# A third Strassen group in the down products of a macaron layer's first SwiGLU, with its post-norm moved to ScalarE

## Chip, cores and metric

The kernel runs on one core of a Trainium2 chip, as one launch. The metric is the device time of the launch in microseconds (us). The engines are called PE (TensorE), DVE (VectorE), ACT (ScalarE), POOL (GpSimd) and SP (SyncE).

## What is computed

One hybrid decoder layer on 256 tokens of width 1024 in float32. Cut to what matters here:

```python
def rmsnorm(x, g):
    return x * lax.rsqrt(jnp.mean(x * x, axis=-1, keepdims=True) + EPS) * g

def swiglu(x, w_gate, w_up, w_down):            # w_gate, w_up: 1024 x 2816; w_down: 2816 x 1024
    return (jax.nn.silu(x @ w_gate) * (x @ w_up)) @ w_down

h = h + 0.5 * rmsnorm(swiglu(rmsnorm(h, ffn1_pre_g), ...ffn1...), ffn1_post_g)
u = rmsnorm(h, mix_pre_g)
# the mixer: u @ w_in, a Mamba-2 branch and a differential attention branch, gated, merged, w_out
h = h + rmsnorm(merged @ w_out, mix_post_g)
h = h + 0.5 * rmsnorm(swiglu(rmsnorm(h, ffn2_pre_g), ...ffn2...), ffn2_post_g)
```

The change touches the first SwiGLU ("f1"), its post-norm, and the step from there to the mixer ("mx"). The last SwiGLU ("f2") runs through the same functions.

## The kernel before

**Numbers.** Every product is made of three: each operand is split into a high part (rounded to fp32r by a cast, mostly on ACT) and a low part (the rest, by a subtraction on DVE); high x high, low x high and high x low are accumulated in PSUM. Weights stream from HBM in chunks of 1 MB: SP issues the load into one of three `raw` tiles (`load_to`), two casts on ACT make `whi` (line 251) and two subtractions on DVE make `wlo` (line 254). Once a chunk is split, its raw tile is free, and the load of the third chunk behind it is issued. `take` hands out the next weights and first splits up to three chunks ahead (`AHEAD`).

**Down products.** The 2816 rows of w_down are 11 chunks of 256 rows. In the plan string `DOWN`, "p" is a plain chunk: 2 k-tiles x 2 token blocks x 3 terms x 2 halves of the columns. "q" with a digit is a Strassen group of two chunks: seven products (Winograd's form) instead of eight, each 2 k-tiles x 3 terms of 128 x 512. Its weight operands are four quarters of the two chunks and four sums of them (`Quad.sum_of`, line 123, on DVE); each of the seven operands is split (`wqh`, line 131, on ACT; `wql`, line 136, on DVE). Its activation operands are also sums (`sums_of`), made on DVE while the gate and up products run. `mm_quads` runs the plan up to the last group (line 629), in seven PSUM banks. `combine` adds the banks up on ACT and DVE. `mm_n` (line 577) does the plain chunks behind the last group; it holds the last three (`TAIL`) and does them in the order block 0 left half, block 0 right half, block 1 left, block 1 right, so that block 0 can be normed while block 1 is multiplied.

**Post-norm and the next norm.** When a block of 128 tokens is done, `done` adds the combined parts (line 789) and calls `post_norm`: squares summed on ACT (line 446), a product with the gain on DVE (`og`, line 545), 1/rms, and the update of h on DVE (line 554). 1/rms is `rstd_of` on POOL (lines 451 and 452: an add and a power of -0.5); only the last SwiGLU, where `ready is store`, makes it on ACT as exp(-0.5 ln(x)). Then comes the mixer's norm: the sum of squares of h and 1/rms on POOL (`r_mx`), for block 1 the scaled `un_mx` (line 505), transposes on PE (`pu_mx`, line 460), and their casts and low parts (`u_mx`, lines 466 and 468). Block 0's transposes stand on PE between the left and the right half of block 1. The mixer's first products (`pn_mx`, line 336) are four of 12 matmuls for block 0, with block 1's transposes behind the third, then four for block 1.

**Order.** Tile, the framework, places the instructions of ACT, DVE, POOL and SP (and PE where no order is given) by program order and readiness; each engine then runs its queue in order. From the held chunks to the end of the mixer's first products PE's order is the written one. `add_manual_dep` with `order` is an edge that only bends the order of the queues. In `mm_n` the weights of later chunks are split at two places: up to two chunks ahead behind block 0's norm (`split_to(ahead_of(taken[0], AHEAD - 1))`) and up to three behind block 1's products. ACT has one table of functions loaded at a time; `act_table(EXP_LN)` loads the one with Ln and Exp.

Of the kernel before, what the change touches and what calls it, by code (L numbers as in the profile page):

```python
# [16 lines left out]
F32 = mybir.dt.float32  # L17
F32R = mybir.dt.float32r
AF = mybir.ActivationFunctionType
ALU = mybir.AluOpType  # L20
# [3 lines left out]
EXP_LN = "natural_log_exp_and_others"  # L24
# [16 lines left out]
AHEAD = 3  # L41
# [4 lines left out]
QK_US = 2.4  # L46
GATE_US = 1.75
SSD_US = 1.55
DOWN = {"f1": "p q1 p p q2 p ppp", "f2": "q1 p q2 p q3 ppp"}
FIRST, LAST = (1, 2, 3, 5, 7, 6, 4), (1, 6, 7, 2, 5, 3, 4)  # L50
BREAK, STOP = object(), object()

# [2 lines left out]
def tile_hybrid_layer(ctx: ExitStack, tc: tile.TileContext, x, ffn1_pre_g, ffn1_w_gate, ffn1_w_up,  # L55
# [4 lines left out]
    nc = tc.nc  # L60
# [157 lines left out]
    ffn_chunks("f2", ffn2_w_gate, ffn2_w_up, ffn2_w_down)  # L218

    raws, splits = [], []  # L220
    taken = [0]

    def load_to(n):
# [9 lines left out]
    def split_steps(ahead=True):  # L233


        i, _ = units[len(splits)]
        load_to(i + 1)
        r, shape = raws[i], chunks[i][1]
        nj = shape[1] // 2
        his, los = [], []  # L240
        splits.append((his, los))
        for q in range(2):
            hi = k4([P, nj, shape[2]], f"whi{i}{q}", F32R)
            lo = k4([P, nj, shape[2]], f"wlo{i}{q}", F32R)
            his.append(hi)
            los.append(lo)
            n = 1 if i == 0 else nj
            for j in range(0, nj, n):
                js = slice(j, j + n)
                copy = nc.scalar.copy if i + q + j else nc.vector.tensor_copy  # L250
                copy(hi[:, js, :], r[:, q * nj + j:q * nj + j + n, :])  # L251
                if not i + q + j:
                    yield
                nc.vector.tensor_sub(lo[:, js, :], r[:, q * nj + j:q * nj + j + n, :], hi[:, js, :].bitcast(F32))  # L254
                yield
        raws[i] = None
        if ahead:
            load_to(i + 1 + RAW_BUFS)

    def split_to(n):  # L260

        while len(splits) < min(n, len(units)):
            of, p = units[len(splits)]
            if p is not None:
                splits.append(of.split(p))
                continue
            for _ in split_steps():
                pass

    def ahead_of(i, n):  # L270

        n *= 4
        while n > 0 and i < len(units):
            n -= 4 if units[i][1] is None else 1
            i += 1
        return i
# [72 lines left out]
                between[i + 1]()  # L349


    act_since, act_fence = [], [None]
    order = mybir.DependencyInfo(mybir.DependencyClass.NoSync, mybir.DependencyReason.DATA)

    def act_table(name):
        f = nc.scalar.preload_act_table_set(name)
        for prev in act_since:
            tc.add_manual_dep(f.ins, prev, order, reason="activation table")
        act_since.clear()
        act_fence[0] = f.ins.name  # L360

    def act(*args, **kw):
        a = nc.scalar.activation(*args, **kw)
        if act_fence[0] is not None:
            tc.add_manual_dep(a.ins, act_fence[0], order, reason="activation table")
        act_since.append(a.ins.name)


    order_of, ordered = [ExitStack()], [False]
# [162 lines left out]
        for q in range(2):  # L532
            split(*in_u(b)(q), us[q])

    def post_norm(b, acc, pg, fold, tag, last=False):

        ss = tiny(2, f"sp_{tag}{b}")
        og = []
        for q in range(2):
            sum_sq(ss[:, q:q + 1], acc[q], fold, f"jp_{tag}{b}{q}")  # L540
            if last and q == 0:
                e = tiny(1, f"ep_{tag}{b}")
                nc.vector.tensor_scalar(e, ss[:, 0:1], fold * EPS, None, ALU.add)
            og.append(k2([P, 512], f"og_{tag}{b}{q}"))
            nc.vector.tensor_tensor(og[q], acc[q], pg[:, halves[q]], ALU.mult)
        if last:
            r = tiny(1, f"rp_{tag}{b}")
            act(r, ss[:, 1:2], AF.Ln, bias=e)
            act(r, r, AF.Exp, scale=-0.5)
        else:  # L550
            r = rstd_of(ss, fold, f"rp_{tag}{b}")
        for q in range(2):
            hq = h[:, b, halves[q]]
            nc.vector.scalar_tensor_tensor(hq, og[q], r, hq, ALU.mult, ALU.add)

    def load_gain(v, name):
        pg = k4([P, D], name)
# [3 lines left out]
    def mm_n(acc, acts, ready, turned, begun=lambda: None, pairs=None, begin=True, taken_all=lambda: None):  # L561

        pairs = pairs or range(len(acts) // 2)
        n = len(pairs)
        held = []

        def one(i, w, parts):
            wh, wl = w  # L570
            for kt in range(2):
                ah, al = acts[2 * pairs[i] + kt]
                for b, qs in parts:
                    ts = slice(b * P, (b + 1) * P)
                    for x_, w_ in ((ah, wh), (al, wh), (ah, wl)):
                        for q in qs:
                            nc.tensor.matmul(acc[b][q], x_[:, ts], w_(kt)[:, halves[q]],  # L577
                                             start=begin and i == 0 and kt == 0 and x_ is ah and w_ is wh,
                                             stop=i == n - 1 and kt == 1 and w_ is wl)
                if i == 0:  # L580
                    begun()

        for i in range(n):
            w = take(min(n - i, AHEAD))
            if i < n - TAIL:
                one(i, w, ((0, (0, 1)), (1, (0, 1))))
            else:
                held.append((i, w))
        taken_all()
        own_order(PE)  # L590
        for q in range(2):
            for i, w in held:
                one(i, w, ((0, (q,)),))
        ready(0)
        split_to(ahead_of(taken[0], AHEAD - 1))
        for q in range(2):
            for i, w in held:
                if q == 1 and i == n - TAIL:
                    turned()
                one(i, w, ((1, (q,)),))  # L600
        split_to(ahead_of(taken[0], AHEAD))
        ready(1)

    def sums_of(g, even, odd):

# [129 lines left out]
    def ffn(post_v, tag, ready, turned, then, products):  # L735
        gu = []

        gh = k4([P, 4, T], f"gh_{tag}0", F32R)
        gl = k4([P, 4, T], f"gl_{tag}0", F32R)
        gu += [(gh[:, m, :], gl[:, m, :]) for m in range(4)]  # L740
        sgs = []

        def evict(b, i, acc, r):
            if i == 0:
                sgs.append(k2([P, 512], f"sg_{tag}b{b}"))
                act(sgs[b], acc, AF.Silu, scale=1.0 if r is None else r)
            elif r is None:
                nc.vector.tensor_tensor(sgs[b], acc, sgs[b], ALU.mult)
            else:
                nc.vector.scalar_tensor_tensor(sgs[b], acc, r, sgs[b], ALU.mult, ALU.mult)  # L750

        def back(b):
            bs = slice(b * P, (b + 1) * P)
            pt_ = bg([P, 4, P], f"pt_{tag}{b}")
            for m in range(4):
                nc.tensor.transpose(pt_[:, m, :], sgs[b][:, m * P:(m + 1) * P], ident)
            split(gh[:, :, bs], gl[:, :, bs], pt_)

        products(evict, back)
        back(1)  # L760
        del sgs
        then()
        sums = {}
        for j in range(2, FF // T):
            if j % 2 == 0:
                gh = k4([P, 4, T], f"gh_{tag}{j}", F32R)
                gl = k4([P, 4, T], f"gl_{tag}{j}", F32R)
            o = (j % 2) * 2
            gu += [(gh[:, o + m, :], gl[:, o + m, :]) for m in range(2)]
            sg = k2([P, 2, T], f"sg_{tag}{j}")  # L770
            mm_w(sg, f"pg_{tag}{j}", take(), act_u)
            act(sg, sg, AF.Silu)
            su = k2([P, 2, T], f"su_{tag}{j}")
            mm_w(su, f"pup_{tag}{j}", take(), act_u)
            nc.vector.tensor_tensor(sg, su, sg, ALU.mult)  # L775
            split(gh[:, o:o + 2, :], gl[:, o:o + 2, :], sg)
            if j // 2 in QUADS[tag]:
                if j % 2:
                    sums[j // 2] = sums_of(j // 2, even, sg)
                else:  # L780
                    even = sg
        if ready is store:
            act_table(EXP_LN)
        acc, rest, combine, pairs = mm_quads(gu, sums, tag)
        pg = load_gain(post_v, f"pg_{tag}")

        def done(b):
            for q in range(2):
                nc.vector.tensor_tensor(rest[b][q], acc[b][q], rest[b][q], ALU.add)
            post_norm(b, rest[b], pg, 4.0, tag, ready is store)  # L790
            ready(b)

        mm_n(acc, gu, done, turned, pairs=pairs, begin=False,
             taken_all=combine)

# [176 lines left out]
    pol = const.tile(shp, F32, name="dtp")  # L972
    dt = const.tile(shp, F32, name="dt")

    act_table(EXP_LN)

    lp = const.tile([P, 2, 64], F32, name="lp")
    lvv = lv.rearrange("p (a b) d -> p a b d", b=2)
# [503 lines left out]
```

## Time and profile before

| | us |
|---|---|
| median of 3 runs (lowest to highest) | 735.31 (735.09 to 735.91) |
| profiled execution, its own time | 735.79 |
| its span, from the first instruction to the last | 734.1 |
| PE busy (mean granted clock 0.998) | 725.8 |
| DVE busy | 598.9 |
| ACT busy | 469.4 |

A row of a timeline is: start (us from the span's start), length, engine, line, operation, tiles written <- read, shapes, count, and in brackets the idle time before it and what ended it. A row of the chain of waits, which is followed back from the last instruction, is: start, length, engine, tile, line, count. Tiles are named without their numbers: `acc_f1p` are the down products' banks of the first SwiGLU, `acc_f2p` those of the last.

### The profile page before, as it was taken

The numbers are of one execution on the slowest core, as the hardware profiler recorded it, in microseconds if no ns is written. First come the engines' busy times: TensorE is split into PE (matmuls) and PEld (weight loads), VectorE is DVE, ScalarE is ACT, GpSimd is POOL, SyncE is SP. The second block draws the span as 40 slices with busy tenths as digits, with TensorE's granted clock in tenths as the row PEclk, the third lists the DMA queues.
The fourth block names the chain that finished last, engine by engine and source line by source line (L and its number), as shares of the span: only waits on it lengthen the run. The fifth ranks groups of instructions, "written<-read, shape, count | busy, mean of one in ns | idle before, by whom it ended". The sixth has DMA issues, their size and how long they took to land.

```text
span 734.1 us, 10540 instructions
## 1 busy us (share of the span) xinstructions
PE 725.8 (99%) x4025; PEld 619.3 (84%) x4025; DVE 598.9 (82%) x929; ACT 469.4 (64%) x801; POOL 38.6 (5%) x72
## 2 busy tenths in 40 slices
PE   9999999999999999999999999999999999999996
PEld 7888888888878889999888788888888888888875
DVE  6978777999679999777996997784774878779994
ACT  6666566655567676869965577772663657566562
POOL 2800000000300000000000000000010000000000
PEclk9999999999999999999999999999999999999999
DMA  8874664459353647656564664364460664664541
GB/s 290 239 248 155 225 232 173 129 220 370 119 172 118 191 153 242 212 168 211 157 221 148 208 213 149 138 248 183 135 241 26 230 206 154 214 221 146 185 166 57
DMA packets 94210, 137.92 MB, mean 188 GB/s; under 512 B 2684, under 2 KB 68304, under 8 KB 94160
## 3 DMA queue, kind: packets, MB, share of 16 engines
q1 hardware_dynamic: 91488, 129.51, 52.1%
q0 software_dynamic: 2368, 7.22, 3.1%
q8 instruction: 31, 0.51, 0.3%
q10 hardware_dynamic: 304, 0.53, 0.2%
q14 instruction: 19, 0.16, 0.1%
HBM read 136.17 MB, written 1.08 MB: 187 GB/s over the span
## 4 chain that ended last, share of the span: by engine, by line
PE 97%; DVE 1%; DMA 1%; issue 1%; ACT 0%; SPq 0%; DVEq 0%
PE pup_f L317 9%; PE pg_f L317 9%; PE pws L336 6%; PE pgt L336 6%; PE acc_f1p L629 5%; PE acc_f2p L629 5%; PE pg_f L316 4%; PE pxs L317 4%; PE pup_f L316 4%; PE pn_f L346 3%; PE pn_mx L336 3%; PE acc_mx L577 3%; PE pn_f L336 3%; PE pwd L336 3%; PE acc_f1p L577 3%; PE pz L302 2%
## 5 line engine op out<-in xcount | busy, mean ns | idle before, releaser
L254 DVE TENSOR_TENSOR wlo<-raw,whi 128x1024 fp32r<-128x1024 f32 (+1 forms) x226 | 267.1, 1211 | 21.1 <-ACT whi L251 19.9
L251 ACT CAST whi<-raw 128x1024 fp32r<-128x1024 f32 (+1 forms) x225 | 226.9, 1045 | 15.7 <-DMA raw<-in_w_in_dram 3.4
L317 PE MATMUL pg_f<-u_f,whi 128*128 128x512 f32 x288 | 101.3, 396 | 0.0
L317 PE MATMUL pup_f<-u_f,whi 128*128 128x512 f32 x288 | 101.3, 396 | 0.0
L316 PE MATMUL pg_f<-u_f,wlo 128*128 128x256 f32 x252 | 70.6, 280 | 0.0
L316 PE MATMUL pup_f<-u_f,wlo 128*128 128x256 f32 x252 | 70.3, 279 | 0.0
L317 PEld LDWEIGHTS pup_f<-u_f,whi 128*128 128x128 f32 x288 | 52.8, 188 | 9.8
L317 PEld LDWEIGHTS pg_f<-u_f,whi 128*128 128x128 f32 x288 | 52.8, 188 | 9.7
L316 PEld LDWEIGHTS pg_f<-u_f,wlo 128*128 128x128 f32 x252 | 47.5, 189 | 1.7
L316 PEld LDWEIGHTS pup_f<-u_f,wlo 128*128 128x128 f32 x252 | 47.5, 188 | 1.6
L317 PE MATMUL pxs<-u_mx,whi 128*128 128x512 f32 x128 | 44.6, 397 | 0.0
L322 DVE TENSOR_TENSOR su_f<-pup_f,su_f 128x256 f32<-128x256 f32 x36 | 15.2, 422 | 26.7 <-ACT su_f L321 26.6
L321 ACT COPY su_f<-pup_f 128x256 f32<-128x256 f32 x36 | 13.3, 370 | 36.1 <-PE pup_f L317 35.9
L131 ACT CAST wqh<-wt 128x1024 fp32r<-128x1024 f32 x20 | 21.1, 1054 | 22.8 <-DVE wt L123 17.8
L336 PE MATMUL pgt<-whi,u_mx 128*128 128x512 f32 x128 | 33.1, 393 | 0.0
L302 PE MATMUL pz<-u_mx,whi 128*128 128x256 f32 x128 | 31.8, 285 | 0.0
L303 PE MATMUL pz<-u_mx,whi 128*128 128x256 f32 x128 | 31.4, 283 | 0.0
L316 PE MATMUL pxs<-u_mx,wlo 128*128 128x256 f32 x112 | 31.2, 279 | 0.0
L336 PEld LDWEIGHTS pgt<-whi,u_mx 128*128 128x128 f32 x128 | 23.6, 188 | 5.4 <-issue 0.7
L317 PEld LDWEIGHTS pxs<-u_mx,whi 128*128 128x128 f32 x128 | 23.2, 188 | 4.2
L302 PEld LDWEIGHTS pz<-u_mx,whi 128*128 128x128 f32 x128 | 24.5, 191 | 0.2 <-issue 0.2
L292 ACT CAST gh_f<-sg_f 128x512 fp32r<-128x512 f32 x18 | 11.2, 621 | 21.0 <-DVE sg_f L775 21.0
(402 smaller groups left out, 1681.2 us busy)
## 6 DMA issues: line engine op xcount, KB each, us to landing
raw<-in_w_in_dram SPq DMA_DIRECT2D x40, 1024.0 KB, 5.1
raw<-in_ffn_w_down_dram SPq DMA_DIRECT2D x22, 1024.0 KB, 4.7
raw<-in_ffn_w_gate_dram SPq DMA_DIRECT2D x20, 1024.0 KB, 5.1
raw<-in_ffn_w_up_dram SPq DMA_DIRECT2D x20, 1024.0 KB, 5.0
raw<-in_ssd_w_branch_dram SPq DMA_DIRECT2D x8, 1024.0 KB, 4.8
acb<-acd POOLq DMA_DIRECT2D x8, 512.0 KB, 4.3
raw<-in_da_w_branch_dram SPq DMA_DIRECT2D x4, 1024.0 KB, 4.9
raw<-in_w_out_dram SPq DMA_DIRECT2D x4, 1024.0 KB, 4.8
```

The costliest lines, as they stand in the source:

```text
L131: nc.scalar.copy(hi, src)
L251: copy(hi[:, js, :], r[:, q * nj + j:q * nj + j + n, :])
L254: nc.vector.tensor_sub(lo[:, js, :], r[:, q * nj + j:q * nj + j + n, :], hi[:, js, :].bitcast(F32))
L302: nc.tensor.matmul(acc[m], wh(j)[:, cs], ah(k0 + j), start=first and j == ks[0], stop=False)
L303: nc.tensor.matmul(acc[m], wh(j)[:, cs], al(k0 + j), start=False, stop=False)
L316: nc.tensor.matmul(acc[:, :T], wl(j)[:, cs], ah(j), start=False, stop=False)
L317: nc.tensor.matmul(acc, wh(j)[:, cs], ahl(j), start=j == 0, stop=j == KD - 1)
L322: nc.vector.tensor_tensor(dst[:, m, :], acc[:, :T], dst[:, m, :], ALU.add)
L336: nc.tensor.matmul(acc, a(k0 + j), b(j), start=first and i == 0, stop=last and i == 11)
L346: nc.tensor.matmul(accs[b], x_(k0 + j), w_(j), start=first and j == 0 and w_ is wh and x_ is acts[b][0], stop=last and j == 3 and w_ is wl)
L577: nc.tensor.matmul(acc[b][q], x_[:, ts], w_(kt)[:, halves[q]], start=begin and i == 0 and kt == 0 and x_ is ah and w_ is wh, stop=i == n - ...
L629: nc.tensor.matmul(bank[p], x_, w_, start=p not in begun, stop=last and p in (1, 5, 6, 7))
```

## The change

The first SwiGLU's plan becomes that of the last: three groups and five plain chunks instead of two and seven, the first group first, and three plain chunks behind the last group instead of four. `post_norm` of both SwiGLUs makes 1/rms by Ln and Exp on ACT; the table load for it is written ahead of the down products of both, and the one that was written later, ahead of the mixer's dt, is gone. In `mm_n` the splits behind block 0's norm fall into two: one chunk ahead without a fence, and the second with its low parts behind block 0's last update of h. The third chunk's low parts are behind that too, and its casts behind block 0's Exp. Block 1's adds (`done`) are behind block 0's last update as well. The mixer's own post-norm (`mxp`) stays on POOL and sets no fence.

```diff
-DOWN = {"f1": "p q1 p p q2 p ppp", "f2": "q1 p q2 p q3 ppp"}
+DOWN = {"f1": "q1 p q2 p q3 ppp", "f2": "q1 p q2 p q3 ppp"}
...
+    normed = {"lo": None, "cast": None}
+    def behind(m, what):
+        if normed[what] is not None:
+            tc.add_manual_dep(m.ins, normed[what].name, order, reason="behind a norm")
+        return m
...
-                copy(hi[:, js, :], r[:, q * nj + j:q * nj + j + n, :])
+                behind(copy(hi[:, js, :], r[:, q * nj + j:q * nj + j + n, :]), "cast")
...
-                nc.vector.tensor_sub(lo[:, js, :], r[:, q * nj + j:q * nj + j + n, :], hi[:, js, :].bitcast(F32))
+                behind(nc.vector.tensor_sub(lo[:, js, :], r[:, q * nj + j:q * nj + j + n, :],
+                                            hi[:, js, :].bitcast(F32)), "lo")
...
-    def post_norm(b, acc, pg, fold, tag, last=False):
+    def post_norm(b, acc, pg, fold, tag, scalar=False):
...
-        if last:
+        if scalar:
             r = tiny(1, f"rp_{tag}{b}")
             act(r, ss[:, 1:2], AF.Ln, bias=e)
             act(r, r, AF.Exp, scale=-0.5)
+            last_norm["cast"] = act_last[0]
         else:
             r = rstd_of(ss, fold, f"rp_{tag}{b}")
         for q in range(2):
             hq = h[:, b, halves[q]]
-            nc.vector.scalar_tensor_tensor(hq, og[q], r, hq, ALU.mult, ALU.add)
+            m = nc.vector.scalar_tensor_tensor(hq, og[q], r, hq, ALU.mult, ALU.add)
+            if scalar:
+                last_norm["lo"] = m.ins
...
         ready(0)
+        split_to(ahead_of(taken[0], AHEAD - 2))
+        normed["lo"] = last_norm.get("lo")
         split_to(ahead_of(taken[0], AHEAD - 1))
+        normed.update(last_norm)
...
         split_to(ahead_of(taken[0], AHEAD))
         ready(1)
+        normed.update(lo=None, cast=None)
+        last_norm.clear()
...
-        if ready is store:
-            act_table(EXP_LN)
+        act_table(EXP_LN)
...
-                nc.vector.tensor_tensor(rest[b][q], acc[b][q], rest[b][q], ALU.add)
-            post_norm(b, rest[b], pg, 4.0, tag, ready is store)
+                behind(nc.vector.tensor_tensor(rest[b][q], acc[b][q], rest[b][q], ALU.add), "lo")
+            post_norm(b, rest[b], pg, 4.0, tag, True)
...
-    act_table(EXP_LN)
```

More of the change, by code (lines that the diff above doesn't have):

```diff
@@ L349, in mm_both @@
                 between[i + 1]()
-    act_since, act_fence = [], [None]
+    act_since, act_fence, act_last, last_norm = [], [None], [None], {}
     order = mybir.DependencyInfo(mybir.DependencyClass.NoSync, mybir.DependencyReason.DATA)
@@ L366, in act @@
         act_since.append(a.ins.name)
+        act_last[0] = a.ins
     order_of, ordered = [ExitStack()], [False]
@@ L540, in post_norm @@
             sum_sq(ss[:, q:q + 1], acc[q], fold, f"jp_{tag}{b}{q}")
-            if last and q == 0:
+            if scalar and q == 0:
                 e = tiny(1, f"ep_{tag}{b}")
```

## The prediction

> **What bounds the kernel now.** I read the page's busy line first, then the chain of waits around the two down stages, then the timelines of VectorE (DVE) and ScalarE (ACT) there.
>
> ```profile
> span 734.1 us, 10540 instructions
> PE 725.8 (99%) x4025; PEld 619.3 (84%) x4025; DVE 598.9 (82%) x929; ACT 469.4 (64%) x801; POOL 38.6 (5%) x72
> ...
> 133.40 35.36 PE acc_f1p L629 x156
> 168.76 17.68 PE acc_f1p L577 x78
> 186.45 0.87 PE pu_mx L460 x8
> 187.32 4.10 PE acc_f1p L577 x18
> 191.52 8.23 PE pn_mx L336 x36
> 199.75 0.88 PE pu_mx L460 x8
> 200.62 5.48 PE pn_mx L336 x24
> 206.32 8.20 PE pn_mx L336 x36
> ```
>
> TensorE (PE) is busy for 99% of the span. In the chain, the first SwiGLU's down products (L629, then L577) and the mixer's first products (L336) follow each other with no other engine between them. 156 matmuls in 35.36 us are 0.2267 us each; that pitch, not the modelled duration of one matmul, is the price of one. Before the change this stretch has no stall to win back. Time is saved only by giving PE fewer matmuls, and is lost only by making PE wait.
>
> The second SwiGLU (f2) runs today with the plan that the first is to get. Its chain is the nearest thing to a trace of the change:
>
> ```profile
> 671.18 33.35 PE acc_f2p L629 x147
> 704.57 1.26 DVE wql L136 x2
> ...
> 713.19 1.23 DVE wlo L254
> 714.46 12.78 PE acc_f2p L577 x55
> ...
> 710.02 0.39 PE L577 MATMUL acc_f2p<-whi,gh_f 128*128 128x512 f32 x1
> 714.46 0.50 PE L577 MATMUL acc_f2p<-wlo,gh_f 128*128 128x512 f32 x1 [0.17 <-DVE wlo L254]
> 726.84 0.39 PE L577 MATMUL acc_f2p<-wlo,gh_f 128*128 128x512 f32 x1
> ```
>
> Here the chain leaves PE and runs through DVE from 704.57 to 714.46: the low parts of the weights (wql, wlo) are made only just in time, and the last is late.
>
> **Matmuls.** A plain chunk is 24 matmuls (2 k-tiles, 2 token blocks, 3 terms, 2 halves), a group of two chunks 48. A Strassen group is 7 products of 2 k-tiles by 3 terms, 42. One more group takes 6 matmuls out (252 become 246): 6 x 0.2267 = 1.36 us off PE's path. That is the whole expected gain. The Trainium skill's TensorE: Matmul & The Clock Gate ("Wait — 56ns, not 53.3ns?") measures 215.7 ns start to start for 512 columns; by it the gain would be 1.29. The trace's 0.2267 decides.
>
> **What the group adds on DVE and ACT.** Seven splits stand in place of four: three more casts on ACT, three more low parts and four weight sums (L123) on DVE.
>
> ```profile
> 136.35 1.22 DVE L123 TENSOR_TENSOR wt<-raw,wt 128x1024 f32<-128x1024 f32 x1
> 137.48 1.22 DVE L136 TENSOR_TENSOR wql<-wt,wqh 128x1024 fp32r<-128x1024 f32 x1
> 138.62 1.22 DVE L123 TENSOR_TENSOR wt<-raw,wt 128x1024 f32<-128x1024 f32 x1
> 706.91 4.63 DVE L254 TENSOR_TENSOR wlo<-raw,whi 128x1024 fp32r<-128x1024 f32 x4
> 711.46 0.69 DVE L658 TENSOR_TENSOR u_f<-acc_f2p,p_f 128x512 f32<-128x512 f32 x1
> 712.06 2.35 DVE L254 TENSOR_TENSOR wlo<-raw,whi 128x1024 fp32r<-128x1024 f32 x2
> 710.57 2.00 ACT L251 CAST whi<-raw 128x1024 fp32r<-128x1024 f32 x2 [1.02 <-DMA raw<-in_ffn_w_down_dram]
> ```
>
> The starts are 1.135 us apart, so seven more DVE operations are 7.95 us. They lie beside PE's work only while DVE keeps ahead. In f2 it doesn't quite: between 710.02 and the last start plus one pitch (726.84 + 0.23 = 727.07) lie 17.05 us, and 72 matmuls at 0.2267 are 16.32. The loss is **0.73 us**. It is the last plain chunk's low parts (712.06 x2), held up by its load (ACT sat 1.02 us for it; the load could start only when DVE had released the last group's raw tile) and by the combine's sum at 711.46. The first SwiGLU gets the same plan, buffers and look-ahead, so I charge these 0.73 us there. The bounds are 0 (today's first SwiGLU shows none) and 0.73 plus what the tail below adds.
>
> The activation sums of the third group are hidden. Gate and up products start 11.19 us apart both in the first SwiGLU at a place without sums and in f2 where group 3's are made:
>
> ```profile
> 113.61 0.47 PE pg_f L317 x2
> 124.80 0.47 PE pg_f L317 x2
> 639.71 0.46 PE pg_f L317 x2
> 650.89 0.46 PE pg_f L317 x2
> ```
>
> I cost them at nothing. DMA moves the same bytes. The table load is written earlier but stays one load, so it is also nothing.
>
> **The post-norm.** Two POOL operations per block go; a one-column add on DVE, Ln and Exp come.
>
> ```profile
> 182.40 0.69 DVE L789 TENSOR_TENSOR u_f<-acc_f1p,u_f 128x512 f32<-128x512 f32 x1 [0.39 <-PE acc_f1p L577]
> 185.02 1.42 DVE L554 SCALAR_TENSOR_TENSOR h<-og_f,rp_f,h 128x512 f32<-128x512 f32 x2 [1.20 <-POOL rp_f L452]
> 192.05 0.69 DVE L789 TENSOR_TENSOR c_f<-acc_f1p,c_f 128x512 f32<-128x512 f32 x1
> 195.49 1.42 DVE L554 SCALAR_TENSOR_TENSOR h<-og_f,rp_f,h 128x512 f32<-128x512 f32 x2 [0.84 <-POOL rp_f L452]
> 198.80 1.02 DVE L505 TENSOR_SCALAR un_mx<-h,r_mx 128x512 f32<-128x512 f32 x2 [1.89 <-POOL r_mx L452]
> 719.10 0.69 DVE L789 TENSOR_TENSOR u_f<-acc_f2p,u_f 128x512 f32<-128x512 f32 x1 [1.36 <-PE acc_f2p L577]
> 721.14 1.42 DVE L554 SCALAR_TENSOR_TENSOR h<-og_f,rp_f,h 128x512 f32<-128x512 f32 x2 [0.62 <-ACT rp_f L363]
> 193.65 1.17 POOL L451 TENSOR_SCALAR rp_f<-sp_f 128x1 f32<-128x1 f32 x1 [4.93 <-ACT jp_f L446]
> 197.82 0.30 POOL L451 TENSOR_SCALAR r_mx<-ss_mx 128x1 f32<-128x1 f32 x1 [2.37 <-ACT sq_mx L446]
> 186.40:199.80 13.40, 13.40 (x66) 11.13 (x65) 9.74 (x20) 8.10 (x23) 4.91 (x8) 1.00 0.28 83
> ```
>
> From the last add to the update of h: 2.62 us in block 0 with POOL, 3.44 in block 1, 2.04 with Ln and Exp in f2. The chains get 0.58 and 1.40 us shorter. They gain nothing: the transposes that wait for them (186.45 and 199.75 in the chain) follow PE's previous matmuls with no gap. It is slack, which the rest of the change may use up.
>
> **The fences.** Of the three mixer chunks split in the down stage, today's four plain pairs leave room to make all their low parts before block 0's update. Afterwards the first stays free, the second's and third's low parts (4 x 1.135 = 4.54 us of DVE) come behind it, and the third's casts behind Exp. On DVE's queue they then stand among block 1's add, h and un; behind those wait the transposes at 199.75. Also fenced are block 1's adds: in the timelines they already come after block 0's h, so nothing. The last row above is a window (its length, then busy time of PE, PE's weight loads, DVE, ACT, POOL): DVE is busy 9.74 us of 13.40 between block 0's update and un, which leaves 3.66 us free. I take the fenced low parts at nothing beyond the 0.73: the free time and the slack won by Ln and Exp (3.66 + 1.40 = 5.06) hold the 4.54, narrowly. No row shows their order, so the bounds are 0 and the last rival's 2.4 us.
>
> Two more rows of today's tail, a mixer low part already in front of block 1's norm and DVE's wait for the first casts of the mixer's input, are used further down:
>
> ```profile
> 193.43 1.22 DVE L254 TENSOR_TENSOR wlo<-raw,whi 128x1024 fp32r<-128x1024 f32 x1
> 188.32 2.16 DVE L468 SCALAR_TENSOR_TENSOR u_mx<-pu_mx,cols_a,u_mx 128x128 fp32r<-128x128 f32 x8 [0.41 <-ACT u_mx L466]
> ```
>
> **The sum.** -1.36 + 0.73 = -0.63 us on the profiled execution's 735.79 (735.16). That execution was 0.48 above the median of the runs, 735.31; the forecast is **734.7 us**.
>
> **Rivals.**
> - *DVE in time* (chance 0.32). If the last plain chunk's low parts come before PE asks, the 0.73 goes. The mixer's 96 products then may also run at the 0.2267 pitch: they take 8.23 + 5.48 + 8.20 = 21.91 us now, 21.76 at that pitch, 0.15 more. -1.36 to -1.51, so 733.95 to **733.8**. For it: DVE falls behind in f2 by one operation only, and the release that starts the late load would need to come but 0.7 us earlier. Against it: f2 has the same plan and shows the loss.
> - *The load shared* (0.05). The mixer's chunks now queue behind the last plain chunk's load, where f2 has no later weights. If that costs the load and the low parts as much again, the gain is gone (0.73 twice): **735.4**.
> - *Block 1's norm behind the low parts* (0.29), the side that is slower. Of the 3.66 us that DVE has free, the waits for u_mx's casts (0.41), Ln and Exp (0.62) and r_mx (1.89) are 2.92, so if nothing fits into these waits only 0.74 are usable. 4.54 - 0.74 = 3.80 late, less 1.40 of slack: PE waits 2.40 us at the transposes. With the 0.73 that is -1.36 + 0.73 + 2.40 = +1.77: **737.1**. It decides from a loss of 2.1 us in the tail, that is when more than three of the four low parts get in the way. For it: the changed tail has to place them in a queue that runs in order, and the last one before un already stands in front of an operation of the norm today (193.43). Against it: the mixer's products need the third chunk only after two products, 5.5 us, so the order can be kind.
>
> That low part also ran while POOL's operation at 193.65 took 1.17 us instead of 0.30 at 197.82, where DVE was idle. r_mx stays on POOL, so a low part beside it would cost its chain up to 0.87 us; in the last rival that makes 738.0. The Trainium skill's SBUF — State Buffer ("SBUF: two separate sides") states this as a rule: a DVE operation with two SBUF inputs and a GpSimd operation that reads SBUF lock each other out of a shared port pair for the whole instruction. The two rows agree with it, and it speaks against moving low parts behind the norm.
>
> That the change does not do what it says is left out: the number of matmuls is fixed by the program.
>
> **How the numbers follow.** The forecast has 0.34, its own range 734.2 to 735.3. A measurement of this kernel can tell about 0.2%, or 1.47 us, from no change: 733.84 to 736.78 counts as the same. Of the first rival's 0.32, 0.25 lies beyond 733.84, as 733.8 is at the bound and the runs scatter by some tenths. The last rival's 0.29 counts as slower. So faster 0.25, same 0.07 + 0.34 + 0.05 = 0.46, slower 0.29. The range runs from 733.4 (the first rival less half of the 0.82 us by which the runs of before differ) to 737.4 (the last rival with 0.3 for part of the POOL collision). About 0.2 lies outside, most of it above.
>
> **What would show it.** PE has 6 matmuls fewer in the chain between 133 and 191. A row of an L577 matmul released by "DVE wlo", with some tenths of us and a loss of 0.73 over the last 72 matmuls, confirms the forecast; its absence, the first rival. rp_f is written by ACT (Ln, Exp) and not by POOL, with h waiting about 0.6 us for it. The third mixer chunk's low parts come after block 0's h. The forecast is wrong if the chain shows DVE or ACT for more than 1 us between block 0's update and the mixer's fourth product, above all in front of the second pu_mx.

## The result, and the profile after

| | before | after |
|---|---|---|
| median (lowest to highest), 20 runs each | 735.69 (735.08 to 736.12) | 736.73 (736.14 to 737.48) |
| profiled execution, its own time | 735.79 | 736.73 |
| its span | 734.1 | 735.0 |

The kernel became 1.04 us slower: ratio 1.0014, 95% interval 1.0008 to 1.002. The forecast was 734.7 us, faster by 0.6. The time lies inside the range, and within the 0.2% that was called the same, but on the other side of the kernel before. It is the last rival's upper bound that takes it into the range, not the mechanism of the forecast.

The page after, its span, its busy times and the shares of the chain of waits:

```profile
span 735.0 us, 10551 instructions
PE 725.0 (99%) x4019; PEld 618.1 (84%) x4019; DVE 608.9 (83%) x944; ACT 474.4 (65%) x810; POOL 36.0 (5%) x68
PE 90%; DVE 5%; issue 2%; ACT 2%; DMA 1%; POOL 0%; SPq 0%; DVEq 0%; ACTq 0%; POOLq 0%
```

PE runs six matmuls fewer (4025 before, 4019 now), and the span is nonetheless 0.9 us longer. So more than their price has gone into waits. In the chain PE had 97% of the span before, and has 90% now: DVE (5%), ACT (2%) and the issue times between them have come in. The share alone proves little: e4 below, where PE waits no more than before, has 90% as well. The view of the chain over 158 to 200 us runs through DVE, ACT and POOL almost alone. The view of waits for PE names them (us in total, times, longest):

```profile
PE pu_mx L470 <- DVE un_mx L515: 1.5, 1, 1.5
PE acc_f1p L590 <- DVE wlo L262: 0.2, 1, 0.2
PE acc_f2p L590 <- DVE wlo L262: 0.2, 1, 0.2
```

The second and the third are the loss at the last plain chunk: f2 has had it all along, f1 has it now. The first is new. PE waits for `un_mx`, block 1's normalised input of the mixer. Before, these transposes followed PE's earlier work without a gap. The chain of waits shows what `un_mx` itself waited for:

```profile
190.30 2.36 DVE wlo L262 x2
192.66 0.60 DVE u_f L806
193.26 0.60 DVE c_f L806
193.86 0.60 DVE og_f L555
...
195.31 0.75 DVE h L565
...
196.08 0.68 ACT sq_mx L456 x2
...
197.65 0.73 ACT sq_mx L456 x2
...
198.46 0.71 POOL r_mx L461
...
199.85 0.61 DVE un_mx L515
...
200.51 1.09 PE pu_mx L470 x8
```

Read from below: the transposes at 200.51 follow `un_mx`, that follows r_mx on POOL, the squares on ACT, h, and block 1's two adds (L806). In front of the adds stand two low parts of a mixer chunk. These are no input of the norm; the adds are in the chain behind them only because DVE's queue runs in order. The timeline of DVE and its neighbours gives the places:

```profile
185.53 2.38 DVE L262 TENSOR_TENSOR wlo<-raw,whi 128x1024 fp32r<-128x1024 f32 x2
...
190.30 2.36 DVE L262 TENSOR_TENSOR wlo<-raw,whi 128x1024 fp32r<-128x1024 f32 x2 [0.32 <-ACT whi L259]
192.58 0.68 DVE L806 TENSOR_TENSOR u_f<-acc_f1p,u_f 128x512 f32<-128x512 f32 x1
193.18 0.68 DVE L806 TENSOR_TENSOR c_f<-acc_f1p,c_f 128x512 f32<-128x512 f32 x1
...
199.85 1.02 DVE L515 TENSOR_SCALAR un_mx<-h,r_mx 128x512 f32<-128x512 f32 x2 [0.85 <-POOL r_mx L462]
185.51 1.03 PE L470 MATMUL pu_mx<-ident,h 128*128 128x128 f32 x8
200.51 1.09 PE L470 MATMUL pu_mx<-ident,un_mx 128*128 128x128 f32 x8 [1.54 <-DVE un_mx L515]
```

The low parts at 185.53 are the second mixer chunk's, those at 190.30 the third's. DVE even sat 0.32 us for the third chunk's cast, and block 1's adds came behind that. The two transposes start 15.00 us apart (185.51, 200.51). Before, they were 13.29 apart:

```profile
186.29 1.03 PE L460 MATMUL pu_mx<-ident,h 128*128 128x128 f32 x8
199.58 1.04 PE L460 MATMUL pu_mx<-ident,un_mx 128*128 128x128 f32 x8
```

That is a loss of 1.71 us. The view of waits says 1.5, because it counts from the modelled end of the matmul before. By the starts all 1.71 lie at this place: the last four matmuls ahead of the transposes start at 198.67 in the kernel before and the transposes 0.91 later; here they start at 197.89, and the transposes 2.62 later.

The other loss, at f1's last plain chunk, in the timeline:

```profile
173.07 2.00 ACT L259 CAST whi<-raw 128x1024 fp32r<-128x1024 f32 x2 [1.01 <-DMA raw<-in_ffn_w_down_dram]
173.98 0.68 DVE L676 TENSOR_TENSOR u_f<-acc_f1p,p_f 128x512 f32<-128x512 f32 x1
174.58 2.35 DVE L262 TENSOR_TENSOR wlo<-raw,whi 128x1024 fp32r<-128x1024 f32 x2
176.98 0.50 PE L590 MATMUL acc_f1p<-wlo,gh_f 128*128 128x512 f32 x1 [0.17 <-DVE wlo L262]
```

The first L590 matmul starts at 172.61, and 54 matmuls follow until the first transposes. At 0.2267 us each they are 12.24; the transposes start 12.90 later. The loss is 0.66. All in all: -1.36 + 0.66 + 1.71 = +1.01, against +1.04 between the medians.

### The profile page after: what moved, and what is told of

Read it like the earlier page. It is cut to its first block, busy times and chain, and to the rows that moved or that the text cites. A ratio compares the mean times of both kernels' runs of the same rounds, so it can differ in the third digit from the quotient of the medians.

```text
span 735.0 us, 10551 instructions
## 1 busy us (share of the span) xinstructions
PE 725.0 (99%) x4019; PEld 618.1 (84%) x4019; DVE 608.9 (83%) x944; ACT 474.4 (65%) x810; POOL 36.0 (5%) x68
## 4 chain that ended last, share of the span: by engine, by line
PE 90%; DVE 5%; issue 2%; ACT 2%; DMA 1%; POOL 0%; SPq 0%; DVEq 0%; ACTq 0%; POOLq 0%
PE pg_f L326 9%; PE pup_f L326 9%; PE pws L345 6%; PE pgt L345 6%; PE pg_f L325 4%; PE pxs L326 4%; PE pup_f L325 4%; PE acc_f1p L647 3%; PE acc_f2p L647 3%; PE pn_f L355 3%; PE acc_mx L590 3%; PE pn_f L345 3%; PE pwd L345 3%; PE pz L311 2%; PE pz L314 2%
## 5 line engine op out<-in xcount | busy, mean ns | idle before, releaser
L262 DVE TENSOR_TENSOR wlo<-raw,whi 128x1024 fp32r<-128x1024 f32 (+1 forms) x222 | 262.2, 1209 | 18.8 <-ACT whi L259 17.7
L259 ACT CAST whi<-raw 128x1024 fp32r<-128x1024 f32 (+1 forms) x221 | 222.9, 1044 | 12.4 <-PE psc L1188 2.5
L131 ACT CAST wqh<-wt 128x1024 fp32r<-128x1024 f32 x24 | 25.3, 1053 | 22.2 <-DVE wt L123 22.0
L136 DVE TENSOR_TENSOR wql<-wt,wqh 128x1024 fp32r<-128x1024 f32 x24 | 29.3, 1219 | 0.2
```

Of the source, the lines that this page charges most:

```text
L131: nc.scalar.copy(hi, src)
L136: last_lo[0] = nc.vector.tensor_sub(lo, src, hi.bitcast(F32)).ins
L259: behind(copy(hi[:, js, :], r[:, q * nj + j:q * nj + j + n, :]), "cast")
L262: behind(nc.vector.tensor_sub(lo[:, js, :], r[:, q * nj + j:q * nj + j + n, :], hi[:, js, :].bitcast(F32)), "lo")
```

## The experiments

Every kernel was timed against the kernel before on the same chip, whose median was 735.83 us beside e1 to e4, 735.81 beside e5 to e8 and 736.18 beside e9 and e10. So kernels of different groups are compared by their distance from the kernel before; that of the changed kernel is +1.04 us. Waits are read from one profiled execution of each.

**e1: the third chunk's splits behind block 1's norm in program order.**

```diff
-        split_to(ahead_of(taken[0], AHEAD))
         ready(1)
+        split_to(ahead_of(taken[0], AHEAD))
```

> The changed kernel with one edit: the third mixer chunk is split behind block 1's norm in program order, not ahead of it. Theory 1 (the order of DVE's queue: the third chunk's two low parts, at 190.30 for 2.27 us, stand ahead of block 1's adds, which hold up h, un and the second transposes by 1.71 us): that wait falls to 0.3 us or less, the first pbc matmul starts 1.4 us earlier than in the changed kernel's 217.29, and the time falls from 736.7 to about 735.3. Rival 2 (DVE has too much work there whatever the order): the wait only moves to the third product of the mixer, which needs these low parts; the sum of the waits stays within 0.3 of 1.71 and the time at 736.5 to 737. Rival 3 (ACT's casts between the squares hold up the norm): the adds come earlier but h and un don't; at least 1 us of wait stays.

Measured 735.76 us (735.25 to 736.88, 11 runs), ratio 1.0 (0.9991 to 1.0009): 0.07 below the kernel before, where the changed kernel is 1.04 above it. The view of waits no longer lists PE's wait at the second transposes. DVE's queue in its timeline:

```profile
190.06 0.68 DVE L806 TENSOR_TENSOR u_f<-acc_f1p,u_f 128x512 f32<-128x512 f32 x1
190.84 0.69 DVE L806 TENSOR_TENSOR c_f<-acc_f1p,c_f 128x512 f32<-128x512 f32 x1
192.71 1.22 DVE L262 TENSOR_TENSOR wlo<-raw,whi 128x1024 fp32r<-128x1024 f32 x1
193.84 1.41 DVE L565 SCALAR_TENSOR_TENSOR h<-og_f,rp_f,h 128x512 f32<-128x512 f32 x2
195.17 1.22 DVE L262 TENSOR_TENSOR wlo<-raw,whi 128x1024 fp32r<-128x1024 f32 x1
199.21 1.09 PE L470 MATMUL pu_mx<-ident,un_mx 128*128 128x128 f32 x8
```

The same two low parts now stand behind the adds, one where DVE would wait for Ln and Exp, one where it would wait for r_mx. The first does not fit its gap: h starts 3.00 us after c_f, 2.11 in the changed kernel (193.18, 195.29). The transposes are 13.54 us apart (185.67, 199.21). Thus 1.46 of the 1.71 us belong to the order of these two low parts. The other 0.25 are still a wait for `un_mx`, too short for the view to list: the four matmuls ahead of the transposes start at 198.05, 1.16 before them instead of 0.91, and the first of the two un operations, which start at 198.56, ends near 199.17. In its chain stand that late h and an r_mx of 0.86 us beside a low part (197.01). The profiled execution (736.19) was above its median by 0.43: in f2 a gate sum on DVE came late (0.2 us of PE), and the last low parts had two waits of 0.2 instead of one.

**e2: the changed kernel without its fences.** The two settings of `normed` to an instruction are left out, so `behind` orders nothing.

> The changed kernel without its fences (third group, Ln and Exp stay). Theory 1: block 1's first add now may stand ahead of block 0's update of h on DVE, and PE gives it its bank only after block 1's left half; the first transposes then wait about 0.2 + 0.69 + 0.75 = 1.6 us, the second ones 0.5 us or less; the time is near the changed kernel's, 736.2 to 737. If the fences are the whole cost of the change, both waits are gone and the time is 735.0. Rival 2 (too much DVE work): 1.7 us of waits in all, at either place, 736.7.

Measured 737.63 us (737.33 to 738.57, 7 runs), ratio 1.0028 (1.0017 to 1.0038).

```profile
185.55 0.69 DVE L804 TENSOR_TENSOR u_f<-acc_f1p,u_f 128x512 f32<-128x512 f32 x1
...
186.95 1.32 PE L470 MATMUL pu_mx<-ident,h 128*128 128x128 f32 x8 [1.44 <-DVE h L565]
```

Without fences, block 1's first add stands before block 0's update, and PE waits at the first transposes instead. The second transposes still wait 0.42 us. The fences are therefore no mistake: the time without them is 1.80 us above the kernel before, with them 1.04. The prediction had costed the fence on these adds at nothing, because in the plan of before they come behind h without it; in the new plan they don't.

**e3: the third group alone**, with the norm on POOL and no fences: in the kernel before only the plan string is changed.

```diff
-DOWN = {"f1": "p q1 p p q2 p ppp", "f2": "q1 p q2 p q3 ppp"}
+DOWN = {"f1": "q1 p q2 p q3 ppp", "f2": "q1 p q2 p q3 ppp"}
```

> The kernel before with the third group alone: 1/rms on POOL, no fences. Theory 1: PE loses 0.65 at the last plain chunk's low parts as in the changed kernel, and waits at both transposes, since block 0's chain is 0.58 us and block 1's 1.40 us longer and low parts stand in front of both updates of h: 2 to 4 us in all, 737 to 739. Rival 2: as the changed kernel or up to 0.6 slower, 736.7 to 737.3. If the moved 1/rms and the fences are what costs, 735.0.

Measured 738.24 us (736.86 to 739.18, 6 runs), ratio 1.0033 (1.002 to 1.0045): the group by itself is a loss.

```profile
182.81 1.21 DVE L254 TENSOR_TENSOR wlo<-raw,whi 128x1024 fp32r<-128x1024 f32 x1
183.83 2.12 POOL L451 TENSOR_SCALAR rp_f<-sp_f 128x1 f32<-128x1 f32 x1 [14.47 <-ACT jp_f L446]
184.55 1.22 DVE L254 TENSOR_TENSOR wlo<-raw,whi 128x1024 fp32r<-128x1024 f32 x1
187.44 1.64 PE L460 MATMUL pu_mx<-ident,h 128*128 128x128 f32 x8 [1.67 <-DVE h L554]
189.73 0.63 PE L577 MATMUL acc_f1p<-wlo,gh_f 128*128 128x512 f32 x1
190.16 0.63 PE L577 MATMUL acc_f1p<-whi,gh_f 128*128 128x512 f32 x1
```

The profiled execution was a long one (739.08), and the last two rows show why: after PE's wait the matmuls start 0.43 us apart instead of 0.2267, until 191.44. The granted clock is 0.50 between 188.70 and 191.40, and 1.00 up to 188.20 and from 191.80. The two transposes are 15.19 us apart (187.44, 202.63) with no wait of PE listed between them, 1.90 more than before. The three longest runs of e3 (738.80 to 739.18) have a mean granted clock of 0.996, the other three (736.86 to 737.68) 0.998 or 0.999. So a part of the 2.41 us above the kernel before may be the clock's; but even the shortest run is 1.03 above its median. That the wait brought the clock down is not shown: e8 waits 1.89 us at the same place, and its profiled execution keeps 1.00 there.

A column of 128 numbers took POOL 2.12 us beside the low parts and, between them, the product og_f (183.95). The Trainium skill's SBUF — State Buffer ("SBUF: two separate sides") says that a DVE operation with two SBUF inputs and a POOL operation that reads SBUF exclude each other from a shared port pair for a whole instruction. For POOL's side these rows agree: the operation ends 0.18 us behind the low part of 184.55, and took 0.30 us where DVE is idle (197.82 in the kernel before). That DVE has to wait for POOL no row here shows.

**e4: Ln and Exp alone** in the kernel before.

> The kernel before with Ln and Exp alone in the first SwiGLU's post-norm (two groups, no fences). The prediction's view, that the shorter chain is only slack: h comes 0.6 us earlier in block 0 and up to 1.4 in block 1, PE has no wait before or after, the time is that of before within 0.3 us. Other view, that the chain ended last: 0.6 to 2 us faster.

Measured 735.73 us (735.0 to 737.7, 11 runs), ratio 1.0 (0.9991 to 1.0008). No wait of PE appears or goes, and the transposes are 13.29 us apart as before. The shorter norm is slack and nothing else, as the prediction took it.

**e5: the combine's first sum behind the last plain chunk's low parts**, in both SwiGLUs. It tests whether the sum at 173.98 or the transfer before the cast at 173.07 makes the 0.66 us.

```diff
-            tc.add_manual_dep(m.ins, last_lo[0].name, order, ...)
+            tc.add_manual_dep(m.ins, last_plain[0].name, order, ...)
```

> The changed kernel with one edit: the combine's first sum, u2, is ordered behind the last plain chunk's low parts instead of behind the last quad's, in both SwiGLUs. Theory 1 (losses come from the order of DVE's queue): the last plain chunk's low parts start up to 0.5 us earlier, when their casts end; of the 0.65 us between 172.6 and the first pu_mx only the 0.17 us released by DVE wlo and a rest of the casts remains, a gain of 0.4 to 0.5 us, and the same again in the second SwiGLU, where the changed kernel has the same 0.17 us row at 715.35. The 1.5 us wait at the second pu_mx stays. In all 735.8 us (735.5 to 736.4). Rival (that loss belongs to the casts and the transfer before them, ACT L259 idle 1.01 until its DMA): the low parts start no earlier, and the time is that of the changed kernel, 736.7 (736.3 to 737.1).

Measured 737.18 us (736.5 to 737.67, 11 runs), ratio 1.0015 (1.0006 to 1.0024). In the first SwiGLU theory 1 fails and the rival holds:

```profile
173.54 2.00 ACT L259 CAST whi<-raw 128x1024 fp32r<-128x1024 f32 x2 [1.21 <-DMA raw<-in_ffn_w_down_dram]
174.62 2.36 DVE L262 TENSOR_TENSOR wlo<-raw,whi 128x1024 fp32r<-128x1024 f32 x2 [0.30 <-ACT whi L259]
```

The sum is out of the way, and DVE now waits for the cast, which waits for the transfer. From the first L590 matmul (172.78) to the transposes (185.56) are 12.78 us, where the changed kernel has 12.90. The second transposes come 15.42 us behind the first (185.56, 200.98) instead of 15.00, and the time is 1.37 above the kernel before, more than the changed kernel's 1.04 and a little above the rival's range. That wait is longer because a low part (183.55) now stands in front of block 0's h, which starts at 184.68 and not at 184.20; `un_mx` is 0.48 later (200.33). In f2 single executions scatter too much to tell: from the last up product to the last matmul are 55.74 us here, 55.88 in e6 and 56.22 in e7, that all have this edit, and 56.00 in the changed kernel.

**e6: the edits of e1 and e5 together.**

> The edit of e5 and that of e1 together. Theory 1: the gains add up, since they lie at different waits: 736.7 - 1.0 (e1 as measured) - 0.8 to 0.9 (e5) = 734.9 us (734.3 to 735.3), faster than both kernels; no wait of PE at either pu_mx, and the first pbc starts about 1.8 us earlier than in the changed kernel. Rival (DVE is overbooked between 172 and 200 whatever the order): what is saved at one wait comes up at the next, a new wait of 0.4 us or more at the first or second pu_mx, and the time is 735.5 us or more.

Measured 735.37 us (734.76 to 736.84, 11 runs), ratio 0.9996 (0.9987 to 1.0004). This lies between the two theories, 0.44 below the kernel before. The view lists no wait of PE at either transposes, and no new one behind them, against the rival, though by the starts they are 13.76 us apart; and from the first L590 matmul (172.66) to the transposes (185.47) are 12.81 us, so in f1 next to nothing of e5's expected gain came, as in e5 itself.

**e7: e6, with the third chunk fenced behind block 1's update of h.**

```diff
         ready(1)
+        normed.update(last_norm)
         split_to(ahead_of(taken[0], AHEAD))
```

> As e6, but the fence is kept for one chunk more: the third chunk's low parts wait for block 1's update h as well, so they start near 195.3 instead of 192.7. Theory 1: they then come late for the mixer's third product, whose low-part matmuls start near 197.1 (196.2 for its first whi matmuls), and hold POOL's r_mx: PE waits 0.4 to 1.0 us there or at the second pu_mx, 735.3 to 736.0 us. Rival (behind the norm there is free time enough, so the longer fence is harmless or better): as e6 or less, 734.9 us or below.

Measured 735.37 us (734.8 to 735.85, 11 runs), ratio 0.999 (0.9981 to 0.9998). The rival is right that the longer fence is harmless; the time is e6's, and not the 734.9 or less that the rival named:

```profile
190.92 0.69 DVE L807 TENSOR_TENSOR c_f<-acc_f1p,c_f 128x512 f32<-128x512 f32 x1
194.36 2.40 DVE L262 TENSOR_TENSOR wlo<-raw,whi 128x1024 fp32r<-128x1024 f32 x2
197.61 1.02 DVE L515 TENSOR_SCALAR un_mx<-h,r_mx 128x512 f32<-128x512 f32 x2 [0.85 <-POOL r_mx L462]
199.05 1.03 PE L470 MATMUL pu_mx<-ident,un_mx 128*128 128x128 f32 x8
```

h itself is finished a little after 194.4 instead of 195.3, because nothing stands in its chain, so the low parts start earlier than I had written. `c_f` is 2.26 us earlier than in the changed kernel (193.18) and `un_mx` 2.24 (199.85): the delay of two low parts, 2.36 us, is handed on whole. Both of the third chunk's low parts fit between h and `un_mx` here, and the fourth chunk's two, which run at 196.62 in the changed kernel, now stand behind `un_mx` (198.56). PE does not wait at the second transposes; of the 13.54 us between the two (185.51, 199.05) 0.21 more than before are spent in the first, whose eight matmuls take 1.00 us to the next product instead of 0.79.

**e8: only block 1's adds fenced**, not the later chunks' low parts and casts.

> The changed kernel with only a part of its fences: block 1's adds stay ordered behind block 0's update, but later chunks' low parts and casts are not fenced. Theory 1: a chunk's low parts (2 x 1.2 us) or their casts come ahead of block 0's h again, PE waits 0.6 to 1.5 us at the first pu_mx as without any fence (e2: 1.44 us), 737.0 us (736.5 to 737.8). Rival (the fences on low parts and casts are what makes block 1's norm late): the wait at the second pu_mx falls by 1 us or more and none comes up at the first, 735.5 us.

Measured 739.05 us (738.59 to 739.71, 5 runs), ratio 1.0041 (1.0028 to 1.0053), the slowest of all and beyond the expected range.

```profile
184.53 2.35 DVE L262 TENSOR_TENSOR wlo<-raw,whi 128x1024 fp32r<-128x1024 f32 x2
186.80 1.40 DVE L564 SCALAR_TENSOR_TENSOR h<-og_f,rp_f,h 128x512 f32<-128x512 f32 x2
187.59 1.10 PE L469 MATMUL pu_mx<-ident,h 128*128 128x128 f32 x6 [1.89 <-DVE h L564]
```

Two low parts in front of block 0's h cost PE 1.89 us. Exp comes late as well, 184.80 instead of 183.97, behind a cast of a later chunk. It is the same mechanism one block earlier. Half a fence is worse than none: the place that the add leaves in front of h (0.69 us in e2) is taken by a second low part (1.2). Above e2 are 1.4 us (3.24 and 1.80 from the kernel before); 0.67 of them are there when the mixer's next products (`pbc`) start (218.58 against 217.91); I have not followed the rest.

**e9: the raw tile freed earlier.** e7, and two products of the last group change places, so that the last one that reads the group's second chunk comes earlier.

```diff
-FIRST, LAST = (1, 2, 3, 5, 7, 6, 4), (1, 6, 7, 2, 5, 3, 4)
+FIRST, LAST = (1, 2, 3, 5, 7, 6, 4), (1, 6, 7, 2, 3, 5, 4)
```

> As e7, and the third group's products 3 and 5 change places in its order (1, 6, 7, 2, 3, 5, 4), in both SwiGLUs, so the last reader of the group's second raw chunk ends some 1.1 us earlier and frees the buffer for the last plain chunk's transfer. Theory (what is left of the loss at that chunk, 0.54 to 0.63 us in e5 to e7, is its transfer, which waits for that buffer): the transfer is issued near 167.2 and lands near 172.2, its low parts on DVE wait for no cast, the 0.17 us row of PE goes or stays as the last, and the time from the first L590 matmul to the first pu_mx falls from 12.87 to 12.3 to 12.5 us; as much may come from the second SwiGLU. Time 734.8 us (734.3 to 735.1). Rival (DVE itself is full there, whatever the transfer does): the low parts start no earlier, 735.4 us (735.0 to 735.8).

Measured 734.86 us (734.16 to 735.45, 11 runs) against 736.18 for the kernel before: ratio 0.9983 (0.9974 to 0.9992). It is 1.32 below the kernel before, and beats both kernels.

```profile
163.62 2.35 DVE L136 TENSOR_TENSOR wql<-raw,wqh 128x1024 fp32r<-128x1024 f32 x2
165.89 1.22 DVE L123 TENSOR_TENSOR wt<-raw,wt 128x1024 f32<-128x1024 f32 x1
168.09 5.99 ACT L259 CAST whi<-raw 128x1024 fp32r<-128x1024 f32 x6
169.37 6.90 DVE L262 TENSOR_TENSOR wlo<-raw,whi 128x1024 fp32r<-128x1024 f32 x6
184.88 1.24 PE L470 MATMUL pu_mx<-ident,h 128*128 128x128 f32 x8
198.40 1.04 PE L470 MATMUL pu_mx<-ident,un_mx 128*128 128x128 f32 x8
```

The last reader of the raw tile is the sum at 165.89; SP issues the last transfer near 167.2, where the changed kernel does near 168.3. ACT makes six casts and DVE six low parts without a break. From the first L590 matmul (172.43) to the transposes are 12.45 us instead of 12.90, and 12.87 in e7, which differs in the swapped products alone. ACT's wait for this transfer, 1.34 us in e7, is gone. In f2 the last up product and the last matmul are 55.56 us apart (669.60, 725.16) instead of 56.00 (671.75, 727.75); e10, with the same swap, has 55.51, so both lie below every execution without it. The view of waits lists none for PE from 131 us to the end. By the starts 0.21 us are left ahead of the first transposes and 0.23 between the two (13.52).

**e10: e9 with the first SwiGLU's norm back on POOL.** The adds and low parts stay fenced, the casts are not.

> As e9, but the first SwiGLU's post-norm takes its 1/rms on POOL (two operations of L461 and L462) instead of Ln and Exp on ScalarE, with the adds and the low parts still fenced; the casts are not. Theory (Ln and Exp are worth more here than the slack that e4 showed them in, since POOL's operation lies beside DVE's low parts and takes 0.7 to 2.1 us instead of 0.3): block 0's update comes 1 to 2 us later, PE waits 0.5 to 1.7 us at the first or second pu_mx, and the time is 0.5 to 1.7 us above e9. Rival (the update's place is set by DVE's queue alone, and the norm's engine is of no account): within 0.3 us of e9.

Measured 736.63 us (735.79 to 738.78, 11 runs), ratio 1.0007 (0.9998 to 1.0016), 1.77 above e9. The size is just outside what was expected, and the place is another:

```profile
194.49 1.41 DVE L565 SCALAR_TENSOR_TENSOR h<-og_f,rp_f,h 128x512 f32<-128x512 f32 x2 [0.85 <-POOL rp_f L462]
197.04 0.73 PE L345 MATMUL pn_mx<-whi,u_mx 128*128 128x512 f32 x2 [0.48 <-ACT whi L259]
```

PE waits for the third chunk's cast (0.48 us) and, behind the second transposes, for the fourth chunk's low parts (0.4, at 202.62). From `c_f` (191.75) to h are 2.74 us, against 2.12 in e9 (190.28, 192.40): 0.62 us are POOL's. But PE waits at neither transposes, and POOL's operation at rp_f took 0.45 and 0.46 us (183.12, 193.35), not the 0.7 to 2.1 of the theory. Of the 2.09 us between the two profiled executions 0.57 are there before the first L590 matmul (173.00), ahead of the norm. How much of the 1.77 is the norm and how much the casts that lost their fence isn't told apart.

## Why the prediction was wrong, step by step

- **Six matmuls, -1.36.** Right: the count fell by six, and so did the time of the stretch. From the first matmul of the last up product to the first transposes are 58.65 us before (127.64, 186.29) and 57.53 in e9 (127.35, 184.88). That is 1.12 less, with 0.21 lost over the last 54 matmuls: 1.33 for the six. e9's whole 1.32 is another sum, with some 0.5 us won in f2 (56.06 before, 55.56) and 0.4 still lost around the transposes.
- **+0.73 at f1's last plain chunk.** Right in size and place: 0.66 us, and the row of PE released by "DVE wlo" came as said. Of its two causes, the load and the combine's sum, e5 leaves 0.12 us for the sum, and e9 against e7 shows the load: freeing the raw tile 1.1 us sooner takes 0.42 us off. The row rules out the first rival (DVE in time), and 0.66 instead of twice 0.73 the second (the load shared).
- **Ln and Exp are only slack.** Right (e4). From `c_f` to h were 2.11 us in block 1 after (193.18, 195.29), 2.04 was the estimate. Whether the slack is needed once the third group is there e10 does not show.
- **The sums of the group, DMA and the table load at nothing.** No wait of PE in the changed kernel points to them.
- **"I take the fenced low parts at nothing".** This step failed, by 1.71 us. It held 5.06 us of free time and slack against 4.54 us of low parts, summed over the whole stretch from block 0's update to `un_mx`. But nearly all of DVE's 3.66 us free were waits: 0.41 and 0.42 ahead of block 1's last add, 0.84 (rp_f) and 1.89 (r_mx) behind it. So most of the room lay *behind* the add, and the third chunk's low parts were put *ahead* of it. There they don't use the gaps, they push them along. e1 and e7 put the same low parts behind the adds, and of PE's 1.71 us 0.25 and nothing are left at the second transposes. The sum was too generous besides: in e1 one of the fourth chunk's low parts has moved behind `un_mx` (199.50), in e7 both, so no run shows room for all that it counted, and the low part of 1.2 us at 192.71 in e1 is longer than its gap. What was wrong above all was to take room for order. The sign that the prediction had named came: the chain shows DVE, ACT and POOL from 190.30 to `un_mx`, in front of the second transposes. The program's text had it: the third chunk's split stood before `ready(1)`, and its fence was block 0's update alone.
- **The last rival, block 1's norm behind the low parts (+2.40).** Its mechanism is what happened; the size is 1.71. It charged 3.80 us of low parts to the chain; e7 against the changed kernel shows 2.24 us, the third chunk's two. Those of the second chunk were over at 187.9, while PE's last down product for block 1, without which `c_f` can't be added, starts only at 190.25. The rival gave 2.1 us, or more than three of the four low parts, as the point from which it decides; two low parts have made 1.71, and so a time between the forecast and the rival's.
- **POOL's collision.** r_mx took 0.71 us beside low parts instead of 0.31 at 189.51 in the same trace, 0.4 of the up to 0.87. It is inside the 1.71.
- **The sum.** With the failed step mended and nothing else (e1) the difference to the kernel before is 735.76 - 735.83 = -0.07, by the ratio's interval -0.66 to +0.66. The forecast's -0.63 lies at its edge; the waits in e1's profile would give -1.36 + 0.66 + 0.25 = -0.45. With e5's edit and the longer fence as well (e7) it is 735.37 - 735.81 = -0.44, -0.15 to -1.4. That the forecast would have come out right without the failed step is thus likely, but not shown to a tenth.

## What to carry to other kernels

Free time on an in-order engine counts only if the added work can stand in the gaps, and a piece longer than its gap delays the chain by the rest. Ask of each piece what stands behind it in the queue and when that would have been ready; a fence must bind added work behind the chain's *next* link, not behind the one that is done. And where an operand is late, follow it past its engine to the buffer its load waits for: here the order of that buffer's readers was worth 0.42 us (e9), and moving a sum out of the late operand's way 0.12 (e5).

## What the runs showed of the hardware

POOL's time for the same 128 x 1 operation ran from 0.31 us with no low part beside it (r_mx at 189.51, after) over 0.71 (198.46, after) and 0.86 (r_mx in e1) beside low parts to 2.12 (rp_f in e3). POOL's spans are rough, but in e3 the second operation did start only at 186.03, and PE waited for its outcome. I had put the worst at 1.17.

PE's granted clock can fall to about a half within a launch that otherwise runs at 1.00: to 0.50 from 188.70 to 191.40 in e3's profiled execution, behind a wait of 1.67 us. The changed kernel after 1.54 us and e8 after 1.89 kept 1.00. So such a wait may cost more than its own length, and the view of waits does not list the rest; what sets it off these runs do not show.
